# A decoder step in three token groups: 512, 64 + 768 and 768 tokens in place of 64 + 512, 768 and 768

## The chip, the cores and the metric

The kernel runs on one core of one Trainium2 chip. The metric is the device time of one execution in microseconds; the result is the median of several runs. A profiled execution is separate, and has its own time and span. TensorE is PE below, VectorE DVE, ScalarE ACT, GpSimd POOL, and SyncE SP; SP issues nearly all DMAs here.

## The reference

One layer of a decoder is computed for 2048 prompt tokens and for 64 sample tokens (8 sequences of 8) with the same weights, all in fp32:

- h = rmsnorm(x); one projection h @ w_in of 1024 to 4096 columns, split into eight parts of 512 (queries, keys, values and gates of two kinds of heads, four heads of 128 each).
- Retention heads: rotary on queries and keys, a fixed decay per head, state S = decay * S + k^T v, output q S.
- HGRN2 heads: f = lb + (1 - lb) * sigmoid(h W_f), S = diag(f) S + (1 - f)^T i, output S^T q. The prompt starts from zero states, the samples from states that are given; the new states are outputs.
- A norm per head and a gate, then o @ w_out, added to x.
- x + relu(rmsnorm(x) @ w_up)^2 @ w_down with 4096 hidden columns, and a last rmsnorm.

## The kernel before

**Groups.** The 2112 tokens are worked through in the three groups of `GROUPS`: group 0 has the 64 sample tokens and 512 prompt tokens (T = 576), groups 1 and 2 have 768 prompt tokens each. Activations lie with features on the 128 partitions and tokens along the free dimension, in slabs of `SLAB` = 768 columns; the pool `sl` has `NSLAB` = 46 of them. The pool `ld` has 6 more for what is loaded.

**Precision.** Each factor of a large product is cut into hi (rounded to fp32r) and lo (the rest). A product is three matmuls: hi hi, hi lo and lo hi. For a weight, `weight` loads `raw` (512 KB), ACT makes hi (L269), and `second_part` makes lo (L284) on POOL or DVE. Weights are made two ahead of use. In the stream of weights, number j goes to POOL where `j % 4` isn't 0 and `3 < j`, and otherwise to DVE; entries of the later groups with a third field say it themselves. The weights of the mixing and the output projection are written to DRAM in hi and lo once (`kept`) and loaded again by groups 1 and 2, but for the first four, which each group makes anew.

**Order of work.** Each group goes through `mix` (head by head: projections, `values`, and the recurrence in `mixer`), the output projection, and the FFN. `proj` issues a projection: for each block of 128 rows the three matmuls (L340), each once for every piece of the tokens. A group has two pieces, its halves (288 or 384 columns), and the result lies in the two banks of one `pj` tile. PSUM has two such tiles, and four banks of `pm` (`mm`) for all else. After the matmuls of each of the three products a tick goes by. `later(n, f)` and `at` put other engines' work some ticks ahead; `tick` runs what has come due. So the matmul stream is the clock of the program.

**FFN.** Group 0 has a plain one (`ffn_first`): 8 parts of 4 up-projections (`up_first`) and 8 down-projections (`down_first`), in which part t + 1 is projected up before part t is projected down. Down-projections are added to the residual on DVE (L1215). Beside its last part `norm_in` prepares the next group: for each of 8 blocks of x a hi on ACT, a lo (L526), a square and its sum (L509) on DVE. Groups 1 and 2 take quarter blocks with seven products for eight (`up_quad`, `up`, `down`, matmuls at L1123); they need sums of weight blocks. `plan_sums` makes these during group 0: 15 sets, each of four loads, four additions on DVE (L1273) and four stores of 512 KB, at ticks of its own (`side`). The first set starts 90 ticks after the mixing of group 0, the others follow every 100 ticks:

```python
sets = [(("u", t), W_UQ0 + 4 * t) for t in range(1, NQ)]
sets += [(("d", o, v), W_DQ0 + 4 * (2 * o + v)) for o in range(NO) for v in range(2)]
```

**Sample tokens.** They are in group 0, so its mixing also has the samples' states: 8 loads and 8 stores of each kind, `sample_out` (L734, L737) and `sample_update` (L748 to L758).

Of the kernel before, what the change touches and what calls it, by code (L numbers as in the profile page):

```python
# [15 lines left out]
P = 128  # L16
D = 1024
# [8 lines left out]
FF = 4096  # L26
EPS = 1e-6
C = 128
SLAB = 768
NSLAB = 46  # L30
NLD = 6
LEVELS = (64, 32, 16, 8, 4, 2)
NLV = len(LEVELS) + 2
GAM = [1.0 - 2.0 ** (-5.0 - h) for h in range(H)]


GROUPS = ((NS, 0, 512), (0, 512, 768), (0, 1280, 768))
NT = NS + SEQ
WT = 1024
N_IN, N_OUT, N_UP, N_DN = 32, 8, 32, 32  # L40
# [55 lines left out]
NVEC = V_LB + 2 * H  # L96


def constants():
    c = np.zeros((P, NCONST), np.float64)  # L100
    c[:, C_ID:C_ID + P] = np.eye(P)
    s = np.arange(P)[:, None]
    t = np.arange(P)[None, :]
    sc = DK ** -0.5
    same = (s // SLEN == t // SLEN) & (s < NS) & (t < NS)
    for h, g in enumerate(GAM):
        dec = np.where(s <= t, g ** np.maximum(t - s, 0), 0.0) * sc
        c[:, C_RM + h * P:C_RM + (h + 1) * P] = dec
        c[:, C_RS + h * P:C_RS + (h + 1) * P] = np.where(same, dec, 0.0)
        c[:, C_GQ + h * P:C_GQ + (h + 1) * P] = g ** (t + 1.0)  # L110
        c[:, C_GS + h * NS:C_GS + (h + 1) * NS] = g ** (np.arange(NS) % SLEN + 1.0)
        c[:, C_KS + h] = sc * g ** (P - 1.0 - s[:, 0])
        c[:, C_KSS + h] = np.where(s[:, 0] < NS, sc * g ** (SLEN - 1.0 - s[:, 0] % SLEN), 0.0)
    c[:, C_SM:C_SM + NSEQ] = (s // SLEN == np.arange(NSEQ)[None, :])
    m = np.zeros((P, 2 * NLV, P), np.float32)
    for i, w in enumerate(LEVELS + (1,)):
        lv = (s // (2 * w) == t // (2 * w)) & (s % (2 * w) < w) & (t % (2 * w) >= w)
        m[:, i] = lv
        m[:, NLV + i] = lv & (s < NS) & (t < NS) & (w < SLEN)

    i = LEVELS.index(2)
    m[:, 0], m[:, NLV] = m[:, i] * (s % 2), m[:, NLV + i] * (s % 2)
    m[:, NLV - 1] = s == t
    m[:, 2 * NLV - 1] = (s == t) & (s < NS)
    half = DK // 2
    inv = np.power(10000.0, (-np.arange(half, dtype=np.float32) / np.float32(half)).astype(np.float64)).astype(np.float32)
    pos = np.concatenate([np.tile(PAST + np.arange(SLEN), NSEQ), np.arange(SEQ)]).astype(np.float32)
    ang = (inv[:, None] * pos[None, :]).astype(np.float64)
    cs = np.zeros((P, 2, NT), np.float32)
    cs[:half, 0] = cs[half:, 0] = np.cos(ang)  # L130
    cs[:half, 1] = -np.sin(ang)
    cs[half:, 1] = np.sin(ang)
    return c.astype(np.float32), m.reshape(P, -1), cs.reshape(P, -1)

# [63 lines left out]
class Kernel:  # L200
# [43 lines left out]
    def weight(self, i):  # L244
        n = len(self.stream)
        while self.w_next < min(i + 1 + self.ahead, n):
            j = self.w_next
            e = self.stream[j]
            if e[0] == "p":

                self.wts[j] = tuple(self.wp.tile([P, WT], F32R, tag=tag, name=tag) for tag in ("hi", "lo"))
                for part, kept in zip(self.wts[j], self.kept[e[1]]):
                    self.nc.sync.dma_start(part.bitcast(F32), kept)
                self.w_next += 1
                self.w_load = max(self.w_load, j + 1)
                continue
            while self.w_load <= j or j >= self.n_first and self.w_load <= j + 2 and self.w_load < n:
                if self.stream[self.w_load][0] == "p":
                    break
                k, later = self.w_load, self.w_load >= self.n_first  # L260
                raw = self.raws[k] = self.wp.tile([P, WT], F32, tag="sum" if later and k % 3 else "raw", name="raw",
                                                  bufs=4 if later and k % 3 else 2)
                e = self.stream[k]
                self.fetch(raw, self.sums[e[1]] if e[0] == "s" else self.I["w"][e[1]])
                self.w_load += 1
            raw = self.raws.pop(j)
            hi = self.wp.tile([P, WT], F32R, tag="hi", name="hi")
            lo = self.wp.tile([P, WT], F32R, tag="lo", name="lo")
            self.nc.scalar.copy(hi, raw)  # L269
            self.wts[j] = (hi, lo)  # L270
            self.second[j] = raw
            pool = self.stream[j][2] if len(self.stream[j]) > 2 else j % 4 and 3 < j
            if pool or j < 4:
                self.second_part(j, self.nc.gpsimd if pool else self.nc.vector)
            else:
                self.later(4, self.second_part, j, self.nc.vector)
            self.w_next += 1
        self.second_part(i, self.nc.vector)
        return self.wts[i]
# [51 lines left out]
    def proj(self, g, blocks, acts, pieces=None):  # L331

        pieces = pieces or g.pieces
        T2 = pieces[0][1] - pieces[0][0]
        pj = self.pj.tile([P, 2, 512], F32, tag="pj", name="pj")
        n = len(blocks)
        for j, ((wh, wl), (ah, al)) in enumerate(zip(blocks, acts)):
            for q, (w, a) in enumerate(((wh, ah), (wh, al), (wl, ah))):
# [10 lines left out]
        self.later(lag, second) if lag else second()  # L349

    def v2(self, slab, g):
        return slab[:, :g.T].rearrange("p (h t) -> p h t", h=2)

    def rsqrt(self, out, src, scratch, eps, n=1):

# [11 lines left out]
    def build(self):  # L367
        nc, tc, I = self.nc, self.tc, self.I
        with ExitStack() as ctx:
# [8 lines left out]
            self.w_next = self.w_load = self.w_use = 0  # L378
            self.n_mm = self.n_ticks = 0
            self.raws, self.sums, self.side = {}, {}, deque()  # L380
            self.ordered = True
            self.ahead = 2
            self.wts, self.second, self.kept = {}, {}, {}
            self.blocks = deque()
# [18 lines left out]
            for ns, p0, n in GROUPS:  # L403
                g = type("G", (), {})()
                g.i, g.ns, g.p0, g.n, g.T, g.off = len(gs), ns, p0, n, ns + n, off
                off += g.T
                nch = n // C
                first = nch // 2
                g.pieces = [(0, g.T // 2), (g.T // 2, g.T)]
                g.segs = [list(range(first)), list(range(first, nch))]  # L410
                gs.append(g)
            nc.scalar.dma_start(vec, I["vec"])
# [13 lines left out]
            nc.gpsimd.memset(self.ATs, 0.0)  # L426
            self.lower_bounds(cp)

            for i, g in enumerate(gs):
                nxt = gs[i + 1] if i + 1 < len(gs) else None  # L430
                if i == 0:
                    self.mix(g)
                    self.plan_sums(90, 100)
                    self.out_proj_first(g)
                    self.ffn_first(g, nxt)
                    continue
                if i == 1:
                    self.finish_first(gs[0])
                else:
                    self.finish(gs[i - 1])  # L440
                self.mix(g)
                self.out_proj(g)
                self.ffn(g, nxt)
            nc.sync.dma_start(self.O["ret_p"].rearrange("h d v -> d h v"), self.S[:, :H])
            nc.sync.dma_start(self.O["hg_p"].rearrange("h d v -> d h v"), self.S[:, H:])

    def masks(self):
        for i in range(0, 2 * NLV, 4):
            t = self.load()
            self.fetch(t[:, :4 * P], self.I["msk"][:, i * P:(i + 4) * P])  # L450
            self.nc.gpsimd.tensor_copy(self.msk[:, i:i + 4], t[:, :4 * P].rearrange("p (m t) -> p m t", t=P))

    def lower_bounds(self, cp):
        nc = self.nc
# [22 lines left out]
    def parts(self, src, n):  # L477

        t = self.getr()
        hi, lo = t[:, :n], t[:, SLAB // 2:SLAB // 2 + n]  # L480
        self.nc.scalar.copy(hi, src)
        self.nc.vector.tensor_tensor(out=lo, in0=src, in1=hi.bitcast(F32), op=ALU.subtract)
        return hi, lo
# [4 lines left out]
        self.nc.tensor.matmul(ps, self.ones_r, lo, start=False, stop=True)  # L488

    def halves(self, g, src):  # L490
        T2 = g.T // 2
        return [self.parts(src[:, hf * T2:(hf + 1) * T2], T2) for hf in range(2)]

    def both_sums(self, g, parts):

        out = []
        for hi, lo in parts:
            ps = self.mm(g.T // 2)
            self.column_sums(ps, hi, lo)
            out.append(ps)  # L500
        return out
# [10 lines left out]
    def norm_in(self, g, start=False):  # L512


        nc, T, T2 = self.nc, g.T, g.T // 2
        g.h, g.sq = [], None
        g.starts = ([0] if g.ns else []) + [g.ns + C * c for c in range(g.n // C)]

# [23 lines left out]

        def factor():
            g.rs, ln = self.get(), self.get()
            for hf in range(2):
                sl = slice(hf * T2, (hf + 1) * T2)
                ps = self.mm(T2)
                if start:
                    nc.tensor.matmul(ps, self.ones, g.sq[:, sl], start=True, stop=True)
                else:  # L550
# [40 lines left out]
        self.later(t0 + (0 if start else 20), factor)  # L591
        self.later(t0 + 24, rotary)
        self.later(t0 + 24, factor_t, 0)
        self.later(t0 + 28, factor_t, 3)

    def mix(self, g):
        nc = self.nc
# [92 lines left out]
    def values(self, g, p, b):  # L690
# [1 line left out]
        nc = self.nc  # L692
        w = [self.next_weight(), self.next_weight()]
        b["vs"], b["vc"] = None, []
        for i0 in range(0, len(g.starts), SLAB // 256):
            part = g.starts[i0:i0 + SLAB // 256]
            pj = self.pj.tile([P, 2, 512], F32, tag="pj", name="pjv").rearrange("p a b -> p (a b)")
            v = self.get()
            for i, s in enumerate(part):
# [459 lines left out]
    def scale_residual_first(self, g):  # L1159


        nc, T, T2 = self.nc, g.T, g.T // 2
        x = {"sum": None}

        def square(acc):
# [4 lines left out]

        def mean():
            x["q"] = self.get()
            for hf, ps in enumerate(self.both_sums(g, x["parts"])):
                nc.vector.tensor_scalar(out=x["q"][:, hf * T2:(hf + 1) * T2], in0=ps, scalar1=1.0 / D, scalar2=EPS,
                                        op0=ALU.mult, op1=ALU.add)

        def scale(acc):
# [80 lines left out]
        self.later(4 * KB + 10, factor)  # L1258


    def plan_sums(self, first, every):
        nc, w = self.nc, self.I["w"]
        sets = [(("u", t), W_UQ0 + 4 * t) for t in range(1, NQ)]
        sets += [(("d", o, v), W_DQ0 + 4 * (2 * o + v)) for o in range(NO) for v in range(2)]
        self.side = deque()

        def load(x, i, *names):
# [484 lines left out]
```

## Time and profile before

| | us |
|---|---|
| median of 3 runs | 2607.36 (2606.47 to 2609.86) |
| profiled execution | 2605.96 |
| its span | 2604.1 |
| mixing of group 0 (start to 298.8) | 298.8 |
| output projection of group 0 (to 369.4) | 70.6 |
| FFN of group 0 (to 792.2) | 422.8 |
| mixing of group 1 (to 1135.7) | 343.5 |
| output projection of group 1 (to 1213.2) | 77.5 |
| up- and down-projections of group 1 (to 1690.0) | 476.8 |
| mixing of group 2 (to 2033.7) | 343.7 |
| output projection of group 2 (to 2111.2) | 77.5 |
| up- and down-projections of group 2 (to the end) | 493.0 |

Busy time in a page is the time in which an engine had at least one instruction at work. Matmuls overlap, so the mean ns of one matmul (299 for 288 columns) is longer than the time from one start to the next. That time is read from a stretch without gaps, as its length over its count. "Idle before" names who ended the idle time before an instruction.

### The profile page before, as it was taken

How to read it: one execution, taken by the hardware profiler on the slowest of the kernel's cores; microseconds unless marked ns; L12 is line 12 of the kernel's file. 1: busy time of each engine (PE TensorE's matmuls, PEld its weight loads, DVE VectorE, ACT ScalarE, POOL GpSimd, SP SyncE). 2: the span in 40 equal slices, each digit the busy share in tenths (PEclk: the TensorE clock that was granted, in tenths of full speed). 3: DMA queues.
4: the chain of work that ended last, by engine and by line, in shares of the span. 5: the costliest groups of instructions: out<-in, count | busy, mean ns of one | idle time of the engine just before them, and what ended most of it. 6: DMA issues, size and time to landing. Idle time of an engine off the chain costs nothing.

```text
span 2604.1 us, 41673 instructions
## 1 busy us (share of the span) xinstructions
PE 2562.1 (98%) x16999; PEld 2532.6 (97%) x16999; DVE 1660.8 (64%) x2072; ACT 1161.2 (45%) x1581; POOL 932.4 (36%) x538
## 2 busy tenths in 40 slices
PE   8999999999999999999999999999999999999997
PEld 8999999999999999999999999999999999999997
DVE  6666777554566455565554898775555555559876
ACT  6555442222244444444533544444444355345433
POOL 6555547444435133220222332341333012222322
PEclk9999999999999999999999999999999999999999
DMA  7566676666663322232555745442223326565542
GB/s 255 190 214 200 220 280 250 226 229 247 235 226 117 114 98 98 94 110 82 172 185 179 280 173 190 158 146 98 98 98 110 118 78 190 171 215 205 180 169 81
DMA packets 146689, 441.32 MB, mean 169 GB/s; under 512 B 14785, under 2 KB 36289, under 8 KB 146497
## 3 DMA queue, kind: packets, MB, share of 16 engines
q1 hardware_dynamic: 146352, 438.63, 49.1%
q8 instruction: 134, 2.20, 0.3%
q14 instruction: 59, 0.48, 0.1%
q10 hardware_dynamic: 144, 0.02, 0.0%
HBM read 330.85 MB, written 107.74 MB: 168 GB/s over the span
## 4 chain that ended last, share of the span: by engine, by line
PE 81%; DVE 4%; POOL 2%; issue 2%; ACT 1%; DMA 0%; DVEq 0%; POOLq 0%; ACTq 0%
PE pj L340 34%; PE pd L1123 16%; PE pu L1123 16%; PE pjv L705 5%; PE mm L1123 2%; PE mm L834 1%; PE po L1015 1%; PE mm L1023 1%; PE po L1017 1%; POOL lo L284 1%; DVE slab L509 1%; PE mm L891 1%; PE mm L488 1%; POOL slab L1178 1%; PE mm L487 1%
## 5 line engine op out<-in xcount | busy, mean ns | idle before, releaser
L340 PE MATMUL pj<-slab,hi 128*128 128x288 f32 (+1 forms) x5120 | 1016.2, 316 | 15.9 <-DVE slab L1215 7.2
L284 POOL TENSOR_TENSOR lo<-raw,hi 128x1024 fp32r<-128x1024 f32 x173 | 461.4, 2667 | 1079.4 <-ACT hi L269 993.8
L340 PEld LDWEIGHTS pj<-slab,hi 128*128 128x128 f32 x5120 | 810.9, 189 | 21.7 <-DVE slab L1215 8.1
L269 ACT CAST hi<-raw 128x1024 fp32r<-128x1024 f32 x330 | 347.0, 1051 | 746.9 <-PE pj L340 308.1
L340 PE MATMUL pj<-slab,lo 128*128 128x288 f32 (+1 forms) x2560 | 598.9, 315 | 1.4 <-POOL lo L284 1.2
L1123 PE MATMUL pd<-slab,hi 128*128 128x384 f32 x1792 | 456.9, 335 | 5.8 <-DVE slab L1568 2.1
L340 PEld LDWEIGHTS pj<-slab,lo 128*128 128x128 f32 x2560 | 429.2, 189 | 2.5 <-POOL lo L284 1.5
L1123 PE MATMUL pu<-slab,hi 128*128 128x384 f32 x1600 | 396.2, 334 | 0.0
L1123 PEld LDWEIGHTS pd<-slab,hi 128*128 128x128 f32 x1792 | 324.5, 188 | 7.1 <-DVE slab L1568 2.4
L284 DVE TENSOR_TENSOR lo<-raw,hi 128x1024 fp32r<-128x1024 f32 x157 | 208.3, 1327 | 146.2 <-ACT hi L269 142.9
L1123 PE MATMUL pd<-slab,lo 128*128 128x384 f32 x896 | 300.3, 335 | 0.9 <-POOL lo L284 0.9
L1123 PEld LDWEIGHTS pu<-slab,hi 128*128 128x128 f32 x1600 | 288.1, 188 | 0.0
L1123 PE MATMUL pu<-slab,lo 128*128 128x384 f32 x800 | 256.9, 334 | 0.0
L705 PE MATMUL pjv<-hi,slab 128*128 128x256 f32 x1088 | 208.5, 285 | 0.0
L1324 DVE TENSOR_TENSOR slab<-slab 128x768 fp32r<-128x768 f32 x144 | 162.0, 1140 | 33.4 <-ACT slab L1320 20.9
L705 PEld LDWEIGHTS pjv<-hi,slab 128*128 128x128 f32 x1088 | 173.4, 191 | 1.4
L1123 PEld LDWEIGHTS pd<-slab,lo 128*128 128x128 f32 x896 | 168.7, 188 | 1.5 <-POOL lo L284 1.5
L1320 ACT CAST slab<-slab 128x768 fp32r<-128x768 f32 x144 | 117.9, 833 | 105.4 <-DVE slab L1331 82.9
L705 PE MATMUL pjv<-lo,slab 128*128 128x256 f32 x544 | 153.8, 283 | 0.0
L1123 PEld LDWEIGHTS pu<-slab,lo 128*128 128x128 f32 x800 | 149.3, 188 | 0.0
L1538 DVE TENSOR_TENSOR slab<-pd,slab 128x768 f32<-128x768 f32 x110 | 104.2, 950 | 36.9 <-PE pd L1123 36.8
L1273 DVE TENSOR_TENSOR raw<-raw 128x1024 f32<-128x1024 f32 x60 | 104.8, 1746 | 0.6
(198 smaller groups left out, 3325.2 us busy)
## 6 DMA issues: line engine op xcount, KB each, us to landing
raw<-w SPq DMA_DIRECT2D x270, 512.0 KB, 4.4
u<-ld SPq DMA_DIRECT2D x64, 384.0 KB, 4.6
slab<-u SPq DMA_DIRECT2D x64, 384.0 KB, 5.7
ld<-x SPq DMA_DIRECT2D x32, 384.0 KB, 4.6
y<-slab SPq DMA_DIRECT2D x12, 384.0 KB, 2.7
raw<-su1S SPq DMA_DIRECT2D x8, 512.0 KB, 3.4
raw<-su2S SPq DMA_DIRECT2D x8, 512.0 KB, 4.0
raw<-su3S SPq DMA_DIRECT2D x8, 512.0 KB, 4.0
```

What stands on the lines that cost most here:

```text
L269: self.nc.scalar.copy(hi, raw)
L284: eng.tensor_tensor(out=lo, in0=self.second.pop(j), in1=hi.bitcast(F32), op=ALU.subtract)
L340: self.nc.tensor.matmul(pj[:, i, :T2], w, a[:, c0:c1], start=j == 0 and q == 0, stop=j == n - 1 and q == 2)
L487: self.nc.tensor.matmul(ps, self.ones_r, hi, start=True, stop=False)
L488: self.nc.tensor.matmul(ps, self.ones_r, lo, start=False, stop=True)
L509: (eng or nc.gpsimd).tensor_tensor(out=acc[:, :T], in0=acc[:, :T], in1=t[:, :T], op=ALU.add)
L705: nc.tensor.matmul(pj[:, i * 256:(i + 1) * 256], a[:, s:s + C], ww, start=kb == 0 and q == 0, stop=kb == KB - 1 and q == 2)
L1123: self.nc.tensor.matmul(*a, **k)
L1273: self.tc.keep_in_program_order(nc.vector.tensor_tensor(out=x[into], in0=x[a], in1=x[b], op=op))
L1320: self.nc.scalar.copy(hi[:, :g.T], B[name][:, :g.T])
L1324: self.nc.vector.tensor_tensor(out=lo[:, :g.T], in0=B[name][:, :g.T], in1=hi.bitcast(F32)[:, :g.T], op=ALU.subtract)
L1538: nc.vector.tensor_tensor(out=r, in0=ps, in1=r, op=ALU.add)
```

## The change

- The sample tokens go from the first group to the second. T is 512, 832 and 768. `SLAB` is 832 and `NSLAB` 42.
- A group of at most 512 tokens has one piece. Group 0's projections are then matmuls of 512 columns, half as many, with a result of one bank. Group 1's are of 416 columns.
- In group 0's output projection and FFN (`spread`) two of three projections take a bank of `mm` and the third takes a `pj` tile, so six banks go round.
- Lo parts of weights from number 40 on (`W_UP0`) go to DVE, unless their entry says otherwise: 48 of group 0's 64 FFN weights, and three of the four that groups 1 and 2 each make anew, were on POOL before.
- The weight sums of the up-projection (7 sets) are made in group 0, every 200 ticks; the 8 sets of the down-projection are made in group 1's mixing, from tick 100 on, every 84.
- `values` splits its slices evenly (2 + 2 for 4, 3 + 2 + 2 for 7), `parts` takes two slabs where hi and lo of 512 columns don't fit in one, and the masks come as bytes in one DMA where POOL made bytes of four loads. The host lays out x, the rotary tables and y in the new order of tokens.

The diff, cut to its core:

```diff
-SLAB = 768
-NSLAB = 46
+SLAB = 832
+NSLAB = 42
...
-GROUPS = ((NS, 0, 512), (0, 512, 768), (0, 1280, 768))
+GROUPS = ((0, 0, 512), (NS, 512, 768), (0, 1280, 768))
...
-            pool = self.stream[j][2] if len(self.stream[j]) > 2 else j % 4 and 3 < j
+            pool = self.stream[j][2] if len(self.stream[j]) > 2 else j % 4 and 3 < j < W_UP0
...
-        pj = self.pj.tile([P, 2, 512], F32, tag="pj", name="pj")
+        self.n_proj += 1
+        if self.spread and self.n_proj % 3:
+            pj = self.mm().unsqueeze(1)
+        else:
+            pj = self.pj.tile([P, 2, 512], F32, tag="pj", name="pj")
...
-                g.pieces = [(0, g.T // 2), (g.T // 2, g.T)]
+                g.pieces = [(0, g.T)] if g.T <= 512 else [(0, g.T // 2), (g.T // 2, g.T)]
...
+            sums = [(("u", t), W_UQ0 + 4 * t) for t in range(1, NQ)]
+            sums += [(("d", o, v), W_DQ0 + 4 * (2 * o + v)) for o in range(NO) for v in range(2)]
             for i, g in enumerate(gs):
                 nxt = gs[i + 1] if i + 1 < len(gs) else None
                 if i == 0:
                     self.mix(g)
-                    self.plan_sums(90, 100)
+                    self.plan_sums(sums[:NQ - 1], 90, 200)
+
+                    self.spread = True
                     self.out_proj_first(g)
                     self.ffn_first(g, nxt)
+                    self.spread = False
                     continue
                 if i == 1:
                     self.finish_first(gs[0])
+                    self.plan_sums(sums[NQ - 1:], 100, 84)
                 else:
                     self.finish(gs[i - 1])
                 self.mix(g)
+                while self.side:
+                    self.side.popleft()[1]()
                 self.out_proj(g)
                 self.ffn(g, nxt)
...
     def masks(self):
-        for i in range(0, 2 * NLV, 4):
-            t = self.load()
-            self.fetch(t[:, :4 * P], self.I["msk"][:, i * P:(i + 4) * P])
-            self.nc.gpsimd.tensor_copy(self.msk[:, i:i + 4], t[:, :4 * P].rearrange("p (m t) -> p m t", t=P))
+        self.fetch(self.msk.rearrange("p m t -> p (m t)"), self.I["msk"])
...
-        for i0 in range(0, len(g.starts), SLAB // 256):
-            part = g.starts[i0:i0 + SLAB // 256]
+
+        left = -(-len(g.starts) // 3)
+        i1 = 0
+        while left:
+            i0, i1 = i1, i1 - (i1 - len(g.starts)) // left
+            left -= 1
+            part = g.starts[i0:i1]
```

More of the change, by code (lines that the diff above doesn't have):

```diff
@@ L96, with in_groups @@
 NVEC = V_LB + 2 * H
+def in_groups(sample, prompt):
+    out = []
+    for ns, p0, n in GROUPS:
+        out += [sample[:ns], prompt[p0:p0 + n]]
+    return np.concatenate(out, 0)
 def constants():
@@ L126, in constants @@
     inv = np.power(10000.0, (-np.arange(half, dtype=np.float32) / np.float32(half)).astype(np.float64)).astype(np.float32)
-    pos = np.concatenate([np.tile(PAST + np.arange(SLEN), NSEQ), np.arange(SEQ)]).astype(np.float32)
+    pos = in_groups(np.tile(PAST + np.arange(SLEN), NSEQ), np.arange(SEQ)).astype(np.float32)
     ang = (inv[:, None] * pos[None, :]).astype(np.float64)
@@ L132, in constants @@
     cs[half:, 1] = np.sin(ang)
-    return c.astype(np.float32), m.reshape(P, -1), cs.reshape(P, -1)
+    return c.astype(np.float32), m.astype(np.uint8).reshape(P, -1), cs.reshape(P, -1)
 def in_blocks():
@@ L351, in v2 @@
     def v2(self, slab, g):
-        return slab[:, :g.T].rearrange("p (h t) -> p h t", h=2)
+        return slab[:, :g.T].rearrange("p (h t) -> p h t", h=len(g.pieces))
     def rsqrt(self, out, src, scratch, eps, n=1):
@@ L380, in build @@
             self.raws, self.sums, self.side = {}, {}, deque()
-            self.ordered = True
+            self.ordered, self.spread, self.n_proj = True, False, 0
             self.ahead = 2
@@ L479, in parts @@
         t = self.getr()
-        hi, lo = t[:, :n], t[:, SLAB // 2:SLAB // 2 + n]
+        hi, lo = t[:, :n], t[:, SLAB // 2:SLAB // 2 + n] if 2 * n <= SLAB else self.getr()[:, :n]
         self.nc.scalar.copy(hi, src)
@@ L490, in halves @@
     def halves(self, g, src):
-        T2 = g.T // 2
-        return [self.parts(src[:, hf * T2:(hf + 1) * T2], T2) for hf in range(2)]
+        return [self.parts(src[:, c0:c1], c1 - c0) for c0, c1 in g.pieces]
     def both_sums(self, g, parts):
         out = []
-        for hi, lo in parts:
-            ps = self.mm(g.T // 2)
+        for (c0, c1), (hi, lo) in zip(g.pieces, parts):
+            ps = self.mm(c1 - c0)
             self.column_sums(ps, hi, lo)
@@ L512, in norm_in @@
     def norm_in(self, g, start=False):
-        nc, T, T2 = self.nc, g.T, g.T // 2
+        nc, T = self.nc, g.T
         g.h, g.sq = [], None
@@ L544, in factor @@
             g.rs, ln = self.get(), self.get()
-            for hf in range(2):
-                sl = slice(hf * T2, (hf + 1) * T2)
-                ps = self.mm(T2)
+            for hf, (c0, c1) in enumerate(g.pieces):
+                sl = slice(c0, c1)
+                ps = self.mm(c1 - c0)
                 if start:
@@ L593, in norm_in @@
         self.later(t0 + 24, factor_t, 0)
-        self.later(t0 + 28, factor_t, 3)
+        for i in range(3, len(g.starts), 3):
+            self.later(t0 + 25 + i, factor_t, i)
     def mix(self, g):
@@ L1159, in scale_residual_first @@
     def scale_residual_first(self, g):
-        nc, T, T2 = self.nc, g.T, g.T // 2
+        nc, T = self.nc, g.T
         x = {"sum": None}
@@ L1172, in mean @@
             x["q"] = self.get()
-            for hf, ps in enumerate(self.both_sums(g, x["parts"])):
-                nc.vector.tensor_scalar(out=x["q"][:, hf * T2:(hf + 1) * T2], in0=ps, scalar1=1.0 / D, scalar2=EPS,
+            for (c0, c1), ps in zip(g.pieces, self.both_sums(g, x["parts"])):
+                nc.vector.tensor_scalar(out=x["q"][:, c0:c1], in0=ps, scalar1=1.0 / D, scalar2=EPS,
                                         op0=ALU.mult, op1=ALU.add)
@@ L1258, in finish_first, with plan_sums @@
         self.later(4 * KB + 10, factor)
-    def plan_sums(self, first, every):
+    def plan_sums(self, sets, first, every):
         nc, w = self.nc, self.I["w"]
-        sets = [(("u", t), W_UQ0 + 4 * t) for t in range(1, NQ)]
-        sets += [(("d", o, v), W_DQ0 + 4 * (2 * o + v)) for o in range(NO) for v in range(2)]
         self.side = deque()
@@ L1700 @@
     a = {k: np.asarray(v) for k, v in inputs.items()}
-    x = np.concatenate([a["x_sample"].reshape(NS, D), a["x_prompt"].reshape(SEQ, D)], 0)
+    x = in_groups(a["x_sample"].reshape(NS, D), a["x_prompt"].reshape(SEQ, D))
     parts, off = [], 0
@@ L1737 @@
     y = r["y"]
-    rows, off = [], 0
+    samples, prompts, off = [], [], 0
     for ns, p0, n in GROUPS:
         T = ns + n
-        rows.append(y[:, KB * off:KB * (off + T)].reshape(P, KB, T).transpose(2, 1, 0).reshape(T, D))
+        rows = y[:, KB * off:KB * (off + T)].reshape(P, KB, T).transpose(2, 1, 0).reshape(T, D)
+        samples.append(rows[:ns])
+        prompts.append(rows[ns:])
         off += T
-    y = np.concatenate(rows, 0)
     return (
-        y[NS:].reshape(1, SEQ, D),
-        y[:NS].reshape(NSEQ, SLEN, D),
+        np.concatenate(prompts, 0).reshape(1, SEQ, D),
+        np.concatenate(samples, 0).reshape(NSEQ, SLEN, D),
         r["ret_p"].reshape(1, 1, H, DK, DK),
```

## The prediction, made before the changed kernel ran

> **What bounds the kernel now.** I read the page's busy shares first, then stretches cut at the stage boundaries, then PE's waits, then the groups by shape, and last DVE's timeline at the hand-over from group 0 to group 1.
>
> ```profile
> PE 2562.1 (98%) x16999; PEld 2532.6 (97%) x16999; DVE 1660.8 (64%) x2072; ACT 1161.2 (45%) x1581; POOL 932.4 (36%) x538
> ```
>
> PE is busy in 98% of the span, so its idle time (2604.1 - 2562.1 = 42 us) is all that better overlap could give. More must come out of the matmul stream itself. The stretches (us; busy and count of PE, PEld, DVE, ACT, POOL; clock; DMA share; GB/s) give the price of one matmul:
>
> ```profile
> 298.80:369.40 70.60, 67.17 (x498) 64.34 (x497) 51.20 (x78) 27.76 (x44) 20.91 (x11) 1.00 0.90 306
> 369.40:792.20 422.80, 414.51 (x3088) 412.34 (x3086) 251.91 (x202) 131.73 (x168) 217.25 (x97) 1.00 0.64 228
> 792.20:1135.70 343.50, 342.37 (x2388) 337.87 (x2387) 197.99 (x317) 158.30 (x235) 122.47 (x86) 1.00 0.29 106
> 1213.20:1451.80 238.60, 238.60 (x1378) 238.60 (x1377) 135.35 (x133) 111.65 (x130) 60.52 (x23) 1.00 0.55 178
> 455.00:520.00 65.00, 65.00 (x490) 65.00 (x489) 33.12 (x27) 17.92 (x22) 28.55 (x13) 1.00 0.64 226
> ```
>
> In order: group 0's output projection, its FFN, group 1's mixing, group 1's up-projection, and a full stretch of group 0's FFN. The last has 490 matmuls of 288 columns without a gap: 65.00/490 = 132.7 ns each. The up-projection has 384 columns: 238.60/1378 = 173.1 ns. The slope is 40.4/96 = 0.421 ns a column and the line leaves 11.5 ns per matmul that no column pays. The timeline has three of 256 columns every 0.36 us, 120 ns each; the line says 119.2. So a matmul costs about 11.5 ns + 0.421 ns a column.
>
> PE's waits (who waited for whom: us in total, times, longest):
>
> ```profile
> PE pj L340 <- DVE slab L1215: 7.2, 5, 2.8
> PE pj L340 <- ACT hi L269: 6.1, 1, 6.1
> PE pj L340 <- DVE slab L1151: 2.4, 2, 1.6
> PE pj L340 <- POOL lo L284: 1.2, 1, 1.2
> ```
>
> L1215 and L1151 are evacuations of group 0's projections: PE stood because both `pj` tiles were full, 9.6 us in all. 6.1 us is the start. The groups by shape that the change touches:
>
> ```profile
> L340 PE MATMUL pj<-slab,hi 128*128 128x288 f32 x3072 | 549.8, 299 | 14.8 <-ACT hi L269 6.1 <-DVE slab L1215 6.1 <-DVE slab L1151 2.4
> L284 POOL TENSOR_TENSOR lo<-raw,hi 128x1024 fp32r<-128x1024 f32 x173 | 461.4, 2667 | 1079.4 <-ACT hi L269 993.8 <-DVE slab L1538 59.3 <-DMA ld<-x 14.4
> L284 DVE TENSOR_TENSOR lo<-raw,hi 128x1024 fp32r<-128x1024 f32 x157 | 208.3, 1327 | 146.2 <-ACT hi L269 142.9 <-PE mm L1023 2.5
> L1273 DVE TENSOR_TENSOR raw<-raw 128x1024 f32<-128x1024 f32 x60 | 104.8, 1746 | 0.6
> ```
>
> And DVE's timeline where group 0 ends (start, us):
>
> ```profile
> 743.10 1.21 DVE L1273 TENSOR_TENSOR raw<-raw 128x1024 f32<-128x1024 f32 x1
> 760.83 0.94 DVE L509 TENSOR_TENSOR slab<-slab 128x768 f32<-128x768 f32 x1
> 762.63 3.13 DVE L509 TENSOR_TENSOR slab<-slab 128x768 f32<-128x768 f32 x1
> 765.69 0.74 DVE L1215 TENSOR_TENSOR slab<-pj,slab 128x576 f32<-128x576 f32 x1
> ```
>
> And POOL's in the same stretch:
>
> ```profile
> 762.23 2.72 POOL L284 TENSOR_TENSOR lo<-raw,hi 128x1024 fp32r<-128x1024 f32 x1 [3.73 <-ACT hi L269]
> ```
>
> The same L509 takes 0.94 us, or 3.13 where POOL's L284 runs beside it; L1273 takes 1.21 us here against a mean of 1.75. An evacuation (L1215) that is queued behind such a piece is late, and PE waits.
>
> **Widths.** Group 0 has 4608 matmuls of 288 columns at L340 (3072 and 1536 in the groups by shape): 4608 x 132.7 = 611.5 us. With one piece of 512 there are 2304. 512 columns in this type are not in the trace. The line gives 173.1 + 128 x 0.421 = 227.0 ns, so 523.0 us: -88.5. Bounds: the columns alone, 215.6 ns (496.7 us), and 288's price in proportion, 235.9 ns (543.5 us). I take the line, because three widths lie on it. Group 1 has 1536 matmuls of projections, 1368 up and 1344 down, whose width goes from 384 to 416: 4248 x 13.5 ns = +57.3. Net -31.2 (-57.5 to -10.7).
>
> The Trainium skill ("TensorE: Matmul & The Clock Gate", Back-to-back issue gap) gives N/2.4 + 2.5 ns, that is 122.5, 162.5 and 215.8 ns for 288, 384 and 512 columns. The trace is 10 ns above it at both widths it has. By the page alone the two terms were -67.2 and +56.6, and the sum of widths -10.6 instead of -31.2.
>
> **Work that only moves.** The sample tokens' matmuls (busy 15.6 us at L737, 15.0 at L751) go from group 0's mixing to group 1's. The slices of `values` stay 17 in all (4 + 7 + 6 for 5 + 6 + 6). Column sums stay within a few. All of it is PE work in either place: 0.
>
> **Six banks.** A down-projection will last 12 x 227 = 2.7 us and an up-projection 5.4. With two banks an evacuation may be late by one projection, with six by five (13.6 us at least). The longest wait was 2.8 us, so the 9.6 us should go. But at the hand-over DVE's norm pieces grow by 8% (832 for 768) and it gets all four weight parts: I keep 1.6 of the 9.6. Term -8 (-9.6 to +3). `mm` banks also serve column sums and transposes; those are few in this stage and wait for an evacuation at most: 0.
>
> **Weight parts on DVE.** In group 0's FFN 48 of 64 leave POOL (2.6 us each) for DVE (1.21 to 1.38): +58 to +66 us on DVE. About 30 of its 56 sums leave (-53), and its other work shrinks by a ninth (-12). So about 250 us stay DVE's, on a stage of some 350 instead of 423: 71%. A part has two weights' time (10.9 us) before PE needs it; raw lands 4.4 us after issue, ACT takes 1.05, DVE 1.4. Cover holds: 0. If it failed, each weight would cost PE what is late, 64 times. Six parts also move at the heads of groups 1 and 2, where DVE is full: +1.
>
> **Sums beside the second mixing.** Eight sets of four L1273 (32 x 1.21 to 1.77 = 39 to 57 us) go into group 1's mixing. That stage is 343.5 us now. It gets 1152 x 13.5 ns = 15.6, one more slice of `values` (96 x 0.12 = 11.5) and the samples' 30: 400. DVE there: 198 x 832/768 = 214, some 34 for the samples (L748 12.7, L755 and L758 5.5 each, scans and masked copies), and the sums: 287 to 306, or 72 to 76% where it was 58%. A sum's parts are loaded 40 ticks (15 us) ahead, so the make itself hardly waits, but each holds DVE 1.2 to 1.8 us ahead of a step that PE's scores wait for; those have 4 ticks or more. On SP each make holds back its store, and behind that stand the loads of kept weights, two weights (18 us) ahead of PE. DMA goes from 106 to about 190 GB/s; 306 was carried in the stretch at 298.8. Price per make 0 to 1.77 us; 56 of them beside group 0's FFN cost less than its 8.3 us of idle PE, under 0.15 each. I take 0.1: +3 (0 to +57).
>
> **Buffers.** 42 slabs instead of 46. Already ACT and DVE wait for slabs that PE still reads (L1320 11.4 us, L1324 11.7 us on PE's `pd`), and PE's `pd` shows 5.8 us of waiting. Four fewer: +2 (0 to +15).
>
> **Start.** x blocks of 512 for 576 columns and one mask load in place of four loads and POOL's four casts (0.6 us each): -0.3 of the 6.1.
>
> **Sum.** -31.2 - 8 + 1 + 3 + 2 - 0.3 = -33.5. The profiled execution took 2605.96 us (span 2604.1, 1.9 around it), so 2572.5; the median, 2607.36, lies 1.4 above it: 2574.
>
> **Rivals.**
> 1. The fixed 11.5 ns vanishes at 512 columns: 2304 x 11.4 = 26 us more, 2548. For: nothing but that a longer matmul can hide more of the weight load. Against: it is the same at 256, 288 and 384. The page's 215.8 ns says the same for 512. 0.08.
> 2. 512 columns cost in proportion, 235.9 ns: +20.5, 2594. Against it the line, too. 0.08.
> 3. The second mixing becomes bound by DVE. Every make delays PE's next score by its whole length: 32 x 1.77 = 57 in place of 3, 2628. It decides the sign from (33 + 3)/32 = 1.1 us of PE time per make. For: DVE at three quarters, in bursts by head, PE takes its queue in order. Against: PE's idle time beside the 198 us of DVE there is 1.1 us now. 0.09. The Trainium skill ("SBUF — State Buffer", Who interferes with whom) has DVE with two SBUF inputs and POOL block each other for whole instructions; the 0.94 against 3.13 us agrees.
> 4. Four slabs too few: ACT, DVE and POOL wait for a release in the second mixing and the down phases, and PE with them: +15, 2589. For: the 23 us of such waits now. Against: they cost PE little. 0.09.
> 5. Six banks change nothing, since DVE's backlog at the hand-over is as long as they bridge: 2582. 0.06.
>
> **Numbers.** The forecast has 0.60 and its own range 2562 to 2588. The range for 8 in 10, 2550 to 2602, takes in rivals 2, 4, 5 and the widths' bounds; rival 3 and part of rival 1 stay out. A measurement of this kernel can tell 0.2% (5.2 us) from no change. Slower by more: rival 3 and a mixture of 2, 3 and 4, 0.10; within: 0.04; faster: 0.86.
>
> **What would show it.** L340 with 512 columns, 2304 of them (some under the name `mm`), every 227 ns; 416-wide ones every 186.6; group 0's FFN near 350 us; no wait of L340 for L1215 over 1 us; group 1's mixing near 400 us with PE idle under 5; L1273 28 times in group 0 and 32 in group 1's mixing. Wrong would make it: a 512-wide matmul off 227 by 8 or more, or PE waiting for DVE in the second mixing by more than 10 us.

## The result, and the profile after

The changed kernel takes 2586.88 us (median of 4 runs, 2586.12 to 2588.02); the kernel before 2607.28 (2606.47 to 2609.86). The ratio is 0.992, with an interval of 0.9903 to 0.9938: 20 us faster, where 33 were forecast. The profiled execution took 2586.12 us, span 2584.3.

The first line of its page, and its stretches cut where stages end (busy and count of PE, PEld, DVE, ACT, POOL; clock; DMA share; GB/s): group 0's mixing, its output projection, its FFN, and group 1's mixing.

```profile
PE 2538.6 (98%) x14689; PEld 2404.1 (93%) x14689; DVE 1688.4 (65%) x2122; ACT 1166.5 (45%) x1575; POOL 772.3 (30%) x480
```

```profile
0.00:255.40 255.40, 235.48 (x1401) 200.55 (x1402) 165.34 (x297) 167.71 (x268) 145.68 (x118) 0.98 0.63 219
255.40:310.30 54.90, 52.51 (x261) 43.26 (x260) 38.98 (x65) 24.98 (x40) 14.65 (x7) 1.00 0.80 285
310.30:661.20 350.90, 350.88 (x1551) 290.07 (x1550) 218.27 (x221) 130.00 (x169) 85.43 (x51) 1.00 0.51 184
661.20:1064.60 403.40, 396.64 (x2636) 383.50 (x2636) 272.30 (x400) 166.23 (x243) 138.75 (x112) 1.00 0.56 192
```

PE is without a gap in the whole of group 0's FFN, but idle for 20 us in group 0's mixing, the one of these with a clock below 1. PE's waits in group 0's mixing (who waited for whom: us in total, times, longest):

```profile
PE mm L970 <- ACT AT L916: 7.6, 3, 3.5
PE pj L352 <- ACT hi L277: 5.9, 1, 5.9
PE mm L913 <- DVE slab L971: 3.0, 1, 3.0
```

The start (L277) is as before; the other two lines are new: retention scores (L970) wait for a PSUM bank that ACT's copies of corners still hold, and the corners' own matmuls (L913) for one that DVE's L971 still reads. In the FFN no wait for an evacuation is left. The stages of both kernels, cut at the same matmuls, beside what the terms of the forecast come to in each:

| us | before | after | difference | forecast |
|---|---|---|---|---|
| group 0: mixing | 298.8 | 255.4 | -43.4 | -63.9 |
| output projection, FFN | 493.2 | 405.6 | -87.6 | -74.4 |
| group 1: mixing | 343.5 | 403.4 | +59.9 | +60.1 |
| output projection | 77.5 | 90.7 | +13.2 | +5.2 |
| up, down | 477.2 | 515.2 | +38.0 | +36.6 |
| group 2 and the end | 914.0 | 913.9 | -0.1 | +3.0 |
| sum | 2604.2 | 2584.2 | -20.0 | -33.4 |

Two stages carry the miss by this table: the mixing of group 0 gave 20 us less than it should, and its FFN with the output projection 13 more. A part of both is booking. The forecast's column puts all of the samples' matmuls into the mixing, but those of the last head lay in the output projection already before: 32 of 128 at L737 and 8 of 32 at L751, 3.90 and 3.76 us. With these 7.7 us put where they lay, the mixing of group 0 gave 12.8 us less than forecast, and its output projection with the FFN 5.5 more. In the same way group 1's output projection has 8 us more than its forecast, since the last head's sample work now falls into it.

### The profile page after: what moved, and what is told of

Its sections match the earlier page's. It is cut to its first block, busy times and chain, and to the rows that moved or that the text cites. A ratio compares the mean times of both kernels' runs of the same rounds, so it can differ in the third digit from the quotient of the medians.

```text
span 2584.3 us, 37190 instructions
## 1 busy us (share of the span) xinstructions
PE 2538.6 (98%) x14689; PEld 2404.1 (93%) x14689; DVE 1688.4 (65%) x2122; ACT 1166.5 (45%) x1575; POOL 772.3 (30%) x480
## 5 line engine op out<-in xcount | busy, mean ns | idle before, releaser
L352 PE MATMUL pj<-slab,hi 128*128 128x416 f32 (+2 forms) x2844 | 742.4, 364 | 6.3 <-ACT hi L277 5.9
L277 ACT CAST hi<-raw 128x1024 fp32r<-128x1024 f32 x330 | 346.7, 1051 | 677.9 <-PE pu L1145 191.6
L292 POOL TENSOR_TENSOR lo<-raw,hi 128x1024 fp32r<-128x1024 f32 x119 | 314.7, 2645 | 933.9 <-ACT hi L277 866.4
L352 PEld LDWEIGHTS pj<-slab,hi 128*128 128x128 f32 x2844 | 514.3, 189 | 39.1 <-ACT hi L277 5.9
L1145 PE MATMUL pd<-slab,hi 128*128 128x416 f32 (+1 forms) x1792 | 469.5, 342 | 5.1 <-DVE slab L1588 3.1
L352 PE MATMUL pj<-slab,lo 128*128 128x416 f32 (+2 forms) x1422 | 435.6, 364 | 0.1
L1145 PE MATMUL pu<-slab,hi 128*128 128x416 f32 (+1 forms) x1600 | 408.1, 342 | 0.0
L292 DVE TENSOR_TENSOR lo<-raw,hi 128x1024 fp32r<-128x1024 f32 x211 | 269.5, 1277 | 188.7 <-ACT hi L277 188.2
L1145 PE MATMUL pd<-slab,lo 128*128 128x416 f32 (+1 forms) x896 | 307.9, 344 | 0.0
L352 PEld LDWEIGHTS pj<-slab,lo 128*128 128x128 f32 x1422 | 259.9, 189 | 17.2 <-issue 1.9
L1145 PE MATMUL pu<-slab,lo 128*128 128x416 f32 (+1 forms) x800 | 264.2, 343 | 0.0
L352 PE MATMUL mm<-slab,hi 128*128 128x512 f32 x740 | 229.5, 390 | 0.0
L1344 DVE TENSOR_TENSOR slab<-slab 128x832 fp32r<-128x832 f32 (+1 forms) x144 | 162.9, 1148 | 37.4 <-ACT slab L1340 18.1
```

The source lines that it names most:

```text
L292: eng.tensor_tensor(out=lo, in0=self.second.pop(j), in1=hi.bitcast(F32), op=ALU.subtract)
L352: self.nc.tensor.matmul(pj[:, i, :T2], w, a[:, c0:c1], start=j == 0 and q == 0, stop=j == n - 1 and q == 2)
L1145: self.nc.tensor.matmul(*a, **k)
L1344: self.nc.vector.tensor_tensor(out=lo[:, :g.T], in0=B[name][:, :g.T], in1=hi.bitcast(F32)[:, :g.T], op=ALU.subtract)
```

## The experiments

Each is an edit of the changed kernel, except one. Line numbers of experiments are those of their own files, a line or two off.

**Regrouping alone.** Two banks, FFN parts on POOL, all sums beside group 0:

```diff
-                    self.spread = True
+                    self.spread = False
-... j % 4 and 3 < j < W_UP0
+... j % 4 and 3 < j
-                    self.plan_sums(sums[:NQ - 1], 90, 200)
+                    self.plan_sums(sums, 90, 100)
-                    self.plan_sums(sums[NQ - 1:], 100, 84)
```

> Only the grouping (512, 64 + 768, 768), its slabs and the byte masks; two banks for projections, FFN weight parts on POOL and all 15 sums beside group 0 as before. Theory A (the gain is the widths; 416 columns cost 189 ns and not 186.6, and group 0's shorter mixing waits some 10 us for its level chain): widths -90 + 66 = -24 us, mixing of group 0 +10, group 0's FFN keeps its 14 us of waiting or a little more: 2593 to 2602. Theory B (the sums beside the second mixing eat the rest of the gain): without them it is no slower than the changed kernel, 2578 to 2587.

2623.51 us (2622.76 to 2626.23), ratio 1.0064 (1.0047 to 1.0081): slower than before, beyond both theories. The FFN of group 0 took 389.1 us where 1536 matmuls of 512 columns need 348. Its stretch, and PE's largest wait in it:

```profile
313.90:703.00 389.10, 365.20 (x1551) 295.77 (x1549) 248.97 (x200) 128.58 (x167) 219.09 (x99) 0.97 0.69 251
```

```profile
PE pj L352 <- DVE slab L1236: 18.5, 12, 3.5
```

So with the rest of the kernel as it was, the widths save nothing: PE waited for evacuations (18.5 us of the 23.9 in which it stood), and ran at a lower clock for a part of the stage (0.97).

**Two banks again.** `self.spread = False`, all else as changed.

> The changed kernel with two pj tiles for every projection of group 0. If the six banks removed the 9.6 us of waits for evacuations: L352 waits for the evacuation again, 6 to 10 us more, 2593 to 2597. If the moved sums and weight parts had already removed them (DVE no longer late): within 2 us of the changed kernel, 2585 to 2589.

2596.53 us (2595.39 to 2597.31): 9.7 more than the changed kernel. The output projection took 58.2 (54.9 in the changed kernel) and the FFN 355.2 (350.9); waits for evacuations are back (3.6 us at L1237, 2.3 at L1173). The banks are worth their term, if the other two parts are there.

**All sums beside group 0.** `plan_sums(sums, 90, 100)`, none beside group 1.

> The changed kernel with all 15 sets of weight sums beside group 0, every 100 ticks. Theory A: the second mixing gets 2 to 4 us shorter (403.4 now) and group 0's FFN, with DVE near 80%, 0 to 8 longer (350.9 now): 2584 to 2592. Theory B: the second mixing loses most of its waiting, 403 to about 395, and the FFN stays: 2577 to 2581.

2584.09 us (2582.43 to 2587.46), ratio 0.9913 (0.9898 to 0.9928). The second mixing fell from 403.4 to 398.1 us: 32 makes cost it 5.3, 0.17 each. The FFN of group 0 went up to 352.6:

```profile
312.70:665.30 352.60, 351.24 (x1550) 289.83 (x1550) 254.04 (x252) 129.68 (x169) 89.21 (x51) 1.00 0.78 281
```

DVE carries 254 us of work there with PE idle for 1.4. Moving the sums was not needed once the parts had left POOL. By medians the gain is 2.8 us; the intervals of the two ratios overlap.

**FFN parts on POOL.** `j % 4 and 3 < j`, all else as changed.

> The changed kernel with three of four FFN weight parts of group 0 on POOL again (and those at the heads of groups 1 and 2). If six banks cover what POOL does to DVE's pace: within 2 us, 2585 to 2589. If the POOL parts cost (DVE's two-input work slowed at the hand-over, later parts): 2 to 6 us more at the hand-over from group 0 to group 1, 2589 to 2593.

2592.70 us (2591.98 to 2593.94), 5.8 more. The FFN took 356.0 us; PE waited 2.9 us in it for DVE's L1176, which makes an input of the FFN, and 1.2 for POOL's parts.

**Six banks alone.** FFN parts on POOL and all sums beside group 0, with six banks.

> The new groups with six banks alone: FFN weight parts of group 0 on POOL and all 15 sums beside group 0, as before. Regrouping without any of the three took 2623.5 us, with a first FFN of 389.1; the changed kernel has 350.7. If six banks bridge the late evacuations by themselves: FFN 352 to 362, 2586 to 2597. If DVE is too slow on average with POOL beside it and 15 sums, no number of banks helps: FFN 370 to 389, 2603 to 2623.

2611.23 us (2608.80 to 2619.13), ratio 1.0017 (1.0007 to 1.0026): no faster than before. By medians the banks alone gain 12.3 us on two banks (2623.51). The FFN took 385.4 in the profile, only 3.7 less than with two banks, but the profiled execution, 2616.53 us, was a long one of ten. Its stretch and PE's three largest waits:

```profile
311.60:697.00 385.40, 365.29 (x1550) 296.12 (x1549) 258.79 (x205) 129.05 (x168) 219.35 (x99) 0.96 0.71 257
```

```profile
PE mm L503 <- ACT slab L497: 6.6, 1, 6.6
PE mm L352 <- POOL lo L292: 3.6, 5, 1.8
PE pj L352 <- POOL lo L292: 3.2, 2, 2.9
```

The waits for evacuations (L1236) are gone; those for weight parts on POOL and for the input of a column sum (L497) are most of what is left. DVE and POOL are busy 259 + 219 = 478 us in 385; in the changed kernel it is 218 + 85 = 304 in 351. The same squaring on DVE (512 columns, both inputs in SBUF), here and in the changed kernel:

```profile
L1223 DVE TENSOR_TENSOR slab<-slab 128x512 f32<-128x512 f32 x32 | 49.6, 1551 | 65.0 <-ACT slab L1222 65.0
```

```profile
L1224 DVE TENSOR_TENSOR slab<-slab 128x512 f32<-128x512 f32 x32 | 27.5, 860 | 0.0
```

The squaring goes with the parts and not with the sums: it takes 1603 ns with the parts on POOL and half of the sums, and 858 with the parts on DVE and all sums beside it (the two runs above). In the changed kernel DVE makes all 64 parts there (82.9 us) and is still less busy, since it has 24 of the 56 sums and its other work runs faster with less of POOL's beside it. That the pair of DVE and POOL bounds the stage without these edits is a reading of these rows; no run shows a bound as such.

The three edits are no sum of terms: left out one at a time they cost 9.7 (banks), 5.8 (parts) and -2.8 us (sums), left out together 36.6. Parts and sums can largely replace each other. From six banks alone (2611.2) moving only the parts gains 27.1 us (to 2584.1), moving only the sums 18.5 (to 2592.7), and both 24.3.

**The old groups with two of the parts.** The kernel before, FFN parts on DVE and 8 sets of sums beside group 1's mixing.

> The kernel before (groups of 64 + 512, 768, 768, two banks) with FFN weight parts of group 0 on DVE and 8 sets of sums beside group 1's mixing. If these two remove the waiting that the regrouped kernel alone shows (38 us) only because 512 columns shorten the stage: here they take out at most the 14 us of waiting in group 0's FFN and add 5 in group 1's mixing: 2596 to 2604. If they are a gain of their own size whatever the width, near what regrouping alone lost (2623.5 to 2586.9): 2570 to 2585.

2596.30 us (2592.94 to 2603.65), ratio 0.9961 (0.9943 to 0.9978). The FFN fell from 422.8 to 412.3, the mixing of group 1 rose by 3.4:

```profile
368.60:780.90 412.30, 412.04 (x3088) 411.47 (x3087) 221.49 (x218) 131.62 (x168) 85.08 (x49) 1.00 0.46 153
```

PE is full there, so parts and sums take out what waiting there was and no more. What is left between this and the changed kernel, 9 us by medians, is the regrouping with its banks; the six runs here spread over 10.7 us.

**The price of a width.** A block of matmuls behind the kernel's end, 48 of each width, each with a weight load:

```diff
+        for n, (cols, offs) in enumerate(BENCH):
+            for half in range(2):
+                ps = self.mm(cols)
+                for j in range(24):
+                    o = offs[j // 3 % 2]
+                    nc.tensor.matmul(ps, w[:, (j % 8) * P:(j % 8 + 1) * P], a[j % 3 == 1][:, o:o + cols],
+                                     start=j == 0, stop=j == 23)
```

> The changed kernel with a block of matmuls added behind its end: 48 of each width from 256 to 512 columns, each with a weight load of its own, the moving operand at two offsets in turn; its whole time says nothing. If a price of 13 ns + N/2.4 holds for all widths, 416 in this block takes 186.3 ns like its neighbours 400 (179.7) and 432 (193.0), and the 189 of the changed kernel belongs to that kernel's slabs. If 416 is off by itself, it takes 189 here too, with whichever offset. If the offset of the second piece (416 columns, no multiple of 64) is what costs, 416 at 0 and 512 takes 186 and 416 at 0 and 416 takes 189; then 288 at 0 and 288 differs from 288 at 0 and 0 as well, and 384 and 448 are on the line.

This was run once, at a clock of 1.00. PE's stretches, each from the first matmul of a width to the first of the next (48 starts): 384, 400, 416 with both offsets 0, 432 and 448 columns.

```profile
2618.15:2626.50 8.35, 8.35 (x50) 1.00 0.00 0
2626.50:2635.27 8.77, 8.77 (x50) 1.00 0.01 2
2653.30:2662.33 9.03, 9.03 (x49) 1.00 0.01 2
2689.68:2698.97 9.29, 9.29 (x49) 1.00 0.00 0
2698.97:2708.70 9.73, 9.73 (x49) 1.00 0.01 2
```

8.35/48 = 174.0 ns, then 182.7, 188.1, 193.5 and 202.7. A line of 13 ns + N/2.4 passes within 0.3 ns of the prices of 288, 384 and 512 columns in the kernels (132.7, 173.1 and 226.4); it would be 173.0, 179.7, 186.3, 193.0 and 199.7 here. 416 columns are 2 to 3 ns off the line by themselves: with four pairs of offsets the block gives 188.3 three times, and 189.1 for 0 and 416, so the offset adds 0.8 at most. 400 and 448 are off by 3, 408 by 3.6 and 480 by 5. 288, 384 and 512 lie on the line within 1 ns here too. Why these widths differ stays open.

**The mixing's parts on DVE too.** No part of group 0 on POOL:

```diff
-... else j % 4 and 3 < j < W_UP0
+... else 0
```

> The changed kernel with the weight parts of group 0's mixing on DVE too (none on POOL before group 1's FFN). If the POOL parts ahead of the exponents in POOL's queue make the level chain late: the waits for ACT's corner copies (7.6 us) go, and with them most of the half clock behind them, mixing of group 0 from 255 to 243 to 249 us, 2574 to 2581 in all. If the chain is late because the stage is too short for it (or DVE becomes what POOL was): mixing of group 0 stays within 3 us of 255, 2583 to 2590.

2570.82 us (2570.29 to 2572.76), ratio 0.9862 (0.9848 to 0.9877): 16 us faster than the changed kernel, and more than either theory gave. The mixing of group 0 took 241.2 us, and of the 7.6 us of waits for L916 0.2 are left:

```profile
0.00:241.20 241.20, 231.12 (x1402) 197.64 (x1403) 174.78 (x319) 166.51 (x268) 91.51 (x97) 1.00 0.68 232
```

Of the 14.2 us that this stage lost, PE's idle time is 9.8 (19.9 to 10.1) and its busy time 4.4, at a clock of 1.00 where it was 0.98.

What had happened stands in the changed kernel's timelines from 51 us (POOL and DVE, then ACT, then PE). The weight part L292 holds POOL for 2.5 us ahead of the exponents L832 and L833; ACT's exponential L837 waits for them, and behind it in ACT's queue the corner copies L916; these hold a `mm` bank that PE's L970 needs. The first exponent is also slow here (L832 takes 1.60 us, and took 0.80 at 48.25), with a weight part on DVE beside it. That is the smaller share: over the stage L832 and L833 take 827 and 932 ns with parts on POOL, and 784 and 866 without.

```profile
51.59 2.52 POOL L292 TENSOR_TENSOR lo<-raw,hi 128x1024 fp32r<-128x1024 f32 x1 [1.68 <-ACT hi L277]
54.07 1.60 POOL L832 TENSOR_TENSOR slab<-slab 128x256 f32<-128x256 f32 x1
53.22 1.98 DVE L292 TENSOR_TENSOR lo<-raw,hi 128x1024 fp32r<-128x1024 f32 x1 [1.36 <-ACT hi L277]
```

```profile
56.32 0.63 ACT L837 ACTIVATE slab<-slab 128x512 f32<-128x512 f32 x1 [3.14 <-POOL slab L833]
56.86 0.40 ACT L916 COPY AT<-mm 64x128 f32<-64x128 f32 x2
```

```profile
57.15 0.71 PE L970 MATMUL mm<-slab 128*128 128x128 f32 x4 [3.53 <-ACT AT L916]
```

**Slower ticks.** In group 0 the mixer's offsets times 1.1:

```diff
-        at = lambda t, fn, *a: self.at(t0 + t, fn, *a)
+        pace = 1.1 if g.i == 0 else 1
+        at = lambda t, fn, *a: self.at(t0 + round(pace * t), fn, *a)
```

> The changed kernel with all of the mixer's ticks in group 0 stretched by 1.1 (a tick of one 512-wide matmul is 0.226 us, one of two 288-wide ones was 0.265). If the level chain is late since ticks became shorter than the work between them: the waits for corner copies shrink by half or more, mixing of group 0 245 to 251 us, 2577 to 2583. If a POOL or DVE instruction ahead in the queue is the cause, stretching moves the wait and doesn't remove it: 2584 to 2592, with the waits elsewhere in the chain.

2582.19 us (2580.20 to 2583.05), 4.7 less; mixing of group 0 248.7. The waits for L916 went here too. The others in this stage grew a little: 3.6 us at L914 (3.0 at L913 in the changed kernel), 2.2 at L505 (1.8) and 1.3 for ACT's L737 (0.4). Both theories have a share: the offsets were also too short, but taking the weight parts off POOL gains more, 16.1 us for 4.7.

**The best of these together.** All of group 0's parts on DVE, all sums beside group 0, six banks.

> The changed kernel with all of group 0's weight parts on DVE, mixing too, and all 15 sums beside group 0. Each was tried alone: -16.1 and -2.8 us. If they add up, since the one acts in the mixing of group 0 (241.2) and the other in that of group 1 (398.1): 2566 to 2570. If the sums now meet the weight parts in DVE's queue and the first FFN gets longer than 353: 2571 to 2576.

2565.23 us (2564.60 to 2566.41), ratio 0.9839 (0.9825 to 0.9854). Mixing of group 0 241.4, its FFN 352.4, mixing of group 1 398.0: they add up (21.7 us in all, for 16.1 and 2.8 alone). It beats both kernels.

## Why the prediction was right or wrong

- **What bounds the kernel:** right. PE's share stayed 98%; its busy time fell by 23.5 us, and its idle time rose from 42.0 to 45.7.
- **512 columns:** right. A gapless stretch of group 0's FFN:

```profile
340.00:640.00 300.00, 300.00 (x1325) 1.00 0.52 186
```

  300.00/1325 = 226.4 ns, forecast 227.0. Rivals 1 and 2 (215.6 and 235.9) fall. The Trainium skill's N/2.4 + 2.5 ns ("TensorE: Matmul & The Clock Gate", Back-to-back issue gap), which that section gives for an isolated gap, doesn't hold in this stream at 512 either: 226.4 less 512/2.4 is 13.1.
- **416 columns:** mis-sized. Group 1's up-projection:

```profile
1155.30:1415.10 259.80, 259.80 (x1377) 257.45 (x1377) 152.74 (x133) 115.52 (x130) 57.93 (x23) 1.00 0.49 166
```

  259.80/1377 = 188.7 ns, for a forecast of 186.6. On 4248 matmuls that is 9 us lost. The line was taken through widths that all lie on it; 416 doesn't.
- **Work that only moves:** the amount held, but not the 0 for its surroundings. Of the 56.2 us that widths, slices, samples and start should take from group 0's mixing (63.9 less the last head's 7.7), 43.4 came. No step of the forecast asked whether the level chain, the mixer's exponents on POOL, ACT and DVE and the corner copies behind them, fits the shorter stage. Before, PE waited once for it (L940 for ACT's L894, 1.2 us); with a fifth of the stage's time forecast to go, the same POOL, ACT and DVE queues came last. Putting the parts on DVE gave 14.2 us back, more than the 12.8 that were missing.
- **Six banks, -8:** the size was near (9.7 in the changed kernel), the reason half wrong. I took the banks to remove the waits and the parts and sums to cost next to nothing. By the runs the banks alone remove the waits for evacuations, but leave the FFN at 385.4 us, since others take their place. Rival 5, by which DVE's backlog outlasts the banks, is near to that kernel, where they gain 12.3 us of the 36.6; what made it not come true are the other two edits, either of which gives most of the rest by itself.
- **Weight parts on DVE, 0:** mis-sized. They gain 5.8 us in the changed kernel, and 27.1 where the sums stay beside group 0. I added up DVE's load by itself (71%; it was 218 of 351 us, 62%) and took POOL as free time. In the forecast's own rows L509 took 0.94 or 3.13 us; that other two-input work of DVE beside POOL could be slowed like it was not carried into the load. The Trainium skill says that a DVE instruction with two SBUF inputs contends with POOL's reads of SBUF ("SBUF — State Buffer", Who interferes with whom); 860 against 1551 ns for the squaring agrees.
- **Sums beside the second mixing, +3:** 5.3. Rival 3 needed 1.1 us per make and got 0.17. PE stood 6.8 us in that stage, where the forecast had said under 5.
- **Buffers, +2:** 0 in group 2, whose work is the same in both kernels, with 42 slabs for 46: its stages differ by under 1 us. In group 1 no run separates the term, but the few us left over there rule out rival 4's 15.

Together, by the table of stages with the last head's samples where they lay: group 0's mixing +12.8, its output projection and FFN -5.5, group 1 +9.2 (416 columns 9, sums 2.3, waits of its down-projections that went -3.3, and 1 that no run assigns), group 2 and the end -3.1. That is the 13.4 us between forecast and result; that it is no more is in part luck, since misses of both signs cancel.

## What to carry to other kernels

When one stage of the bounding engine's work is shortened, redo the load of the other engines for the new length, and of DVE and POOL as a pair where both read two SBUF inputs. Look at what stands in a queue ahead of the steps that the bounding engine waits for: weight work of 2.5 us a piece ahead of exponents of 0.8 us cost 16 us, more than the six banks gave. Edits that relieve the same bottleneck are judged by leaving out one at a time and all at once: the two answers differed by 24 us here.

## What the runs showed of the hardware

A wait costs more than its length. PE's clock in the changed kernel, in the 3 us in which it stood and the 4 us after:

```profile
54.00:57.00 3.00, 0.00 (x0) 1.00 0.55 142
57.00:61.00 4.00, 3.85 (x22) 0.60 0.95 365
```

A granted clock of 0.60 for 4 us is 1.6 us more. Two equal waits of 2.0 us did differently, by PE's timeline and the 4 us after each:

```profile
119.45 0.71 PE L970 MATMUL mm<-slab 128*128 128x128 f32 x4 [2.02 <-ACT AT L916]
180.46 1.02 PE L970 MATMUL mm<-slab 128*128 128x128 f32 x4 [2.01 <-ACT AT L916]
```

```profile
120.00:124.00 4.00, 4.00 (x33) 1.00 0.96 345
181.00:185.00 4.00, 4.00 (x25) 0.61 1.03 400
```

Cut finer, group 0's mixing has three stretches with a clock of 0.50, each 3.41 us long, from 57.83, 180.71 and 245.57 us. Their starts lie 122.88 and 64.86 us apart, 36 and 19 times 3.413. The Trainium skill's free-running activity window of 3413 ns ("TensorE: Matmul & The Clock Gate", What's actually happening) agrees with both figures; a wait would then count by where it falls. The Trainium skill has the slow clock come after an idle window of some 3.4 us (same section), and here a wait of 2.0 us was once enough. No run here tests the rule.

Where PE waits often the clock is a large part of the loss. In the regrouping alone, stretches at 0.50 come to 23.9 us of group 0's FFN, with six banks alone to 27.3. By an estimate of half of each that is 12 and 14 us, of the 38.2 and 34.5 us by which this stage was longer than the changed kernel's.

Not all widths lie on the line of price that 288, 384 and 512 columns share: 400, 416 and 448 cost 2 to 3 ns more each, 480 5 more, and 432 only 0.5.
